# Layer 0's modulation products on TensorE: two steps at a time, eight products in a row

## The chip, the cores and the metric

The kernel runs on one core of a Trainium2 chip. The metric is the device time of one execution in microseconds (us); lower is better. A core has five engines with queues of their own, which run beside each other: TensorE (PE in the profile; its weight loads are PEld), VectorE (DVE), ScalarE (ACT), GpSimd (POOL) and SyncE (SP), which here issues all transfers from HBM. An engine executes its queue in order and waits where an instruction needs something that another engine or a transfer has not finished. The products accumulate in PSUM banks; everything else lies in SBUF.

## What is computed

Two layers of a trunk (pooling mixer, then neighbourhood attention, each followed by a gated MLP with a width-3 convolution) on 256 latent and 256 context tokens of 2048 channels. Each layer is modulated: a matrix of 2048 x 12288 is multiplied with SiLU of a conditioning vector, and the result gives six vectors of 2048 (shift, scale, gate for the mixer and for the MLP):

```python
silu_c, silu_cc = jax.nn.silu(c), jax.nn.silu(c_ctx)
for i in range(DEPTH):                                   # DEPTH = 2
    ml = (silu_c @ w_mod[i] + b_mod[i]).reshape(B, 6, 1, D)
    mc = (silu_cc @ w_mod[i] + b_mod[i]).reshape(6, 1, 1, D)
    a_lat = modulate(rms_norm(h, norm1_g[i]), ml[:, 0], ml[:, 1])
    ...
    h = h + ml[:, 2] * y_lat
    h = h + ml[:, 5] * conv_ffn(modulate(rms_norm(h, norm2_g[i]), ml[:, 3], ml[:, 4]), ...)
```

The change concerns the products `silu_c @ w_mod[0]` and `silu_cc @ w_mod[0]` of layer 0. Layer 1's are made on VectorE (`mod_pairs`, L214) and are not touched.

## The kernel before

**Chunks and steps.** The 12288 columns of a layer's modulation matrix are 24 chunks of 512 columns; chunk ch belongs to vector ch // 4 and to channel group ch % 4. `mod_pe` (L193) computes one chunk of layer 0. It is a generator with four steps g (2048 rows of the matrix are 4 x 4 x 128). In a step, `load` (L123) brings 2048 columns of four row blocks as two transfers of 512 KB each, and four products (L199) follow, one for each row block j. A product has 128 rows, 512 columns of the matrix as moving data, and only 32 columns of stationary data (two are in use, for the latent and the context vector). `tile_position=(0, 32 * j)` puts the four products of a step on the four 32-column strips of TensorE, and their results on the four 32-partition quarters of one PSUM bank; the first transfer of a step serves j = 0 and 1, the second j = 2 and 3. Since the data are 32-bit floats, each product of the source is two records in the trace. After the fourth step ACT copies the bank to SBUF (L204), PE turns it (L209, tile `modt`), DVE adds up the quarters (L211), and `finish_mod` adds the bias. A chunk is called by its number below, a step and transfer as chunk_step: 22_3 are the two transfers of step 3 of chunk 22.

**The order of the chunks.** `mods` (L425) makes, for each channel group g, the chunks g, 4+g, 8+g, 16+g and 12+g, and at last chunks 20 to 23. `need(n)` (L438) drives this generator to step n. Mixer, partial products and modulation of the four groups are interleaved: `mixer(g)` (L446) pools 512 channels on DVE, POOL and ACT and multiplies them with the mixer weights (products `pm`, L490 to L492); `partial(g)` (L516) multiplies these channels with the first eight tiles of layer 0's gate and up weights (products `cg` and `cu`, L551 to L553, for `wcg` and `wcu`; with small products `pwg` and `pwu`, L534, that read the weights as loaded, and their turns `ptg` and `ptu`, L567). While `partial(g)` runs, `between` (L591) calls `need` at a fixed pace and advances `mixer(g + 1)`. After the last group come the gate and up products of tile 8 (`gu0`, L638 to L640, weights `wg_8` and `wu_8`).

**The weights' way.** All weights go through `load`. `split` (L133) then makes two roundings of each for the fp32r products: ACT casts the high part (L145), DVE subtracts it (L147). The modulation products use the loaded tile itself.

**The rooms.** A transfer's tile lies in a room. `stage` (L115) gives rooms in turn: the first of the list is taken and put at its end. Six rooms are always there; `lend` (L111) adds rooms that hold activations later: 12 at first, 8 during groups 0 to 2, and in group 3 four, then none (`LENT`, L41). A transfer into a room waits until the last reader of the room's former content is done. SyncE issues the transfers in one queue and waits in order.

**Who sets the order.** The program is recorded by the Python code and then ordered by the tile framework's scheduler, which estimates times when the program is built and decides the order on each engine; `high_priority` and `issue_after` guide it. So the order in which instructions stand on an engine can change far from an edit. The order is fixed before the program runs.

Of the kernel before, what the change touches and what calls it, by code (L numbers as in the profile page):

```python
# [59 lines left out]
def kernel(ctx: ExitStack, tc: tile.TileContext, xT, cxT, wmod, wg, wu, wd, wp,  # L60
                         wq, wv, wo, vec, cc, rope, inv, strips, out):
    nc = tc.nc
# [8 lines left out]
    def bank(tag, name):  # L71

        if tag == "d" and nbank[0] is not None:
            nbank[0] += 1
            if nbank[0] % 4 == 0:
                tag = "m"
        return pp.tile([P, 512], F32, tag=tag, bufs={"gu": 4, "d": 3, "m": 1}[tag], name=name)
# [37 lines left out]
    def stage(name):  # L115

        r = rooms.pop(0)
        rooms.append(r)
        if r >= 0:
            return ap0.tile([P, 1024], F32, tag=f"A{r}", name=name)  # L120
        return wst.tile([P, 1024], F32, tag=f"wst{-r}", name=name)

    def load(src, cols, name):  # L123

        ts = []
        for j in range(0, cols, 1024):
            n = min(1024, cols - j)
            t = stage(f"{name}_{j}")
            nc.sync.dma_start(t[:, :n], src(j, j + n))
            ts.append((t, n))  # L130
        return ts

# [18 lines left out]
    def ld(src, name, share=0):  # L151
        return split(load(lambda a, b: src[:, a:b], 2048, name), name, share)
# [6 lines left out]
    def mod_tile(l, ch):  # L159

        return main.tile([P, 4, 2], F32, tag=f"modT{ch if ch < 20 else (l, ch)}", name=f"modT{l}_{ch}")

    def by_row(ps):

        return ps.rearrange("p (i j c) -> p i c j", i=4, j=4)[:, :, 0:2, :]
# [9 lines left out]
    def finish_mod(l, ch, streams, src):  # L175

        mt = src[0] if len(src) == 1 else mod_tile(l, ch)
        n = len(streams)
        which, q = divmod(ch, 4)

        def dup(name, a):
            return V(name)[:, a : a + 8].rearrange("p (i s) -> p i s", s=2)[:, :, 0:n]

        bias = dup(f"bm_{l}", 8 * ch)
        for b, v in enumerate(src):
            own = slice(32 * b, 32 * b + 32) if len(src) > 1 else slice(0, P)
            nc.vector.tensor_tensor(mt[own, :, 0:n], v, bias[own], op=ALU.add)
        if which in (1, 4):
            nc.vector.scalar_tensor_tensor(mt[:, :, 0:n], mt[:, :, 0:n], 1.0, dup(f"g{1 if which == 1 else 2}_{l}", 8 * q),
                                           op0=ALU.add, op1=ALU.mult)  # L190
        modT[l, ch] = mt

    def mod_pe(l, ch, sc, pool):  # L193

        ps = bank("m", f"mod{l}_{ch}")
        for g in range(4):
            ts = load(lambda a, b: wmod[l, ch, g, :, a:b], 2048, f"wm{l}_{ch}_{g}")
            for j in range(4):
                nc.tensor.matmul(ps[32 * j : 32 * j + 32, :], sc[:, 4 * g + j, :],  # L199
                                 ts[j // 2][0][:, 512 * (j % 2) : 512 * (j % 2) + 512],  # L200
                                 start=(g == 0), stop=(g == 3), tile_position=(0, 32 * j))
            if g == 3:
                ev = pool.tile([P, 512], F32, tag="t2", name=f"modev{l}_{ch}")
                nc.scalar.copy(ev, ps)  # L204
            yield
        with tc.high_priority():
            p2 = bank("d", f"modt{l}_{ch}")
            for i in range(4):
                nc.tensor.transpose(p2[:, P * i : P * i + P], ev[:, P * i : P * i + P], ident)  # L209
        r = mod_tile(l, ch)  # L210
        nc.vector.tensor_reduce(out=r, in_=by_row(p2), axis=AX.X, op=ALU.add)  # L211
        finish_mod(l, ch, both, [r])
# [116 lines left out]
    with ExitStack() as ph0:  # L329
# [17 lines left out]
        sc = p0.tile([P, KT, 32], F32, name="sc")  # L347
# [44 lines left out]
        with ExitStack() as phs:  # L392
# [16 lines left out]
            for j in range(2):  # L409
                t = st.tile([P, 2, WP], F32, bufs=1, name=f"pad{j}")  # L410
# [3 lines left out]
            for j in range(2):  # L414
                t = st.tile([P, 4, 32], F32, bufs=1, name=f"sh{j}")
# [9 lines left out]
            def mods():  # L425

                for g in range(4):
                    for w in (0, 1, 2, 4):
                        yield from mod_pe(0, 4 * w + g, sc, f0)
                    yield from mod_pe(0, 12 + g, sc, f0)  # L430
                    shifts(g)
                for q in range(4):
                    yield from mod_pe(0, 20 + q, sc, f0)
# [82 lines left out]
            def partial(g, sh, between):  # L516

                step = 0
                for fa in range(0, NS, 4):
                    for q, (nm, wsrc) in enumerate((("g", wg), ("u", wu))):  # L520
                        ts = load(lambda a, b: wsrc[0, fa + a // 512 : fa + b // 512, :, 512 * g : 512 * g + 512]
                                  .rearrange("f p c -> p f c"), 2048, f"wc{nm}{g}_{fa}")
                        parts = split(ts, f"wc{nm}{g}_{fa}")
# [715 lines left out]
```

## Time and profile before

| | |
|---|---|
| runs | 3067.25, 3070.6, 3072.18 us, median 3070.6 |
| the profiled execution's own time | 3070.34 us |
| its span | 3068.5 us |
| mean granted TensorE clock | 0.994 |
| modulation products of layer 0 (L199) | 768 records, 131.1 us of PE's busy time |
| their transfers | 192 of 512 KB |
| idle time of PE before L199 that a transfer ended | 23.3 us |

The span runs from the first to the last instruction of the profiled execution; its own time adds what lies around it. Times in the profile are counted from the span's start. A row of a timeline gives start, duration, engine, line, operation, output <- inputs, shapes, the count of merged records, and in brackets the idle time before it with what ended it. Records of TensorE overlap, since its work is pipelined: the distance between starts says more than the duration.

### The profile page before, as it was taken

The page shows a single profiled execution, that of the slowest core. Times are in us where ns is not written, and L with a number is a line of the kernel's source. Part 1 is how long each engine was busy: PE and PEld are TensorE (multiplying, and loading weights), DVE is VectorE, ACT ScalarE, POOL GpSimd, SP SyncE. Part 2 cuts the span into 40 slices and gives each one's busy share as a digit, 9 for nine tenths or more (in the row PEclk, how much of TensorE's full clock was granted, in tenths as well). Part 3 has the DMA queues.
Part 4 walks back from the last instruction along what each step waited for, and adds up shares of the span by engine and source line. Part 5 has one row for each costly group of instructions (what it writes and reads, how often), then busy time and mean ns, then how long its engine had stood idle before and what let it go on. Part 6 is the DMA issues. An engine that isn't in the chain of part 4 may idle for free.

```text
span 3068.5 us, 40828 instructions
## 1 busy us (share of the span) xinstructions
PE 3007.0 (98%) x15082; PEld 2414.2 (79%) x15082; DVE 1939.4 (63%) x2748; ACT 1372.9 (45%) x2219; POOL 826.4 (27%) x823
## 2 busy tenths in 40 slices
PE   6999999999999999999999999999999999999998
PEld 2565658888888888888887888878888888888887
DVE  4445774285674857658485666474767666666666
ACT  3333454423333242433334444343545666666665
POOL 2011213303022130311302000000002566566665
PEclk9999999999999999999999999999999999999999
DMA  9878663284755747466482333333355556565553
GB/s 382 334 271 305 215 233 103 90 253 141 223 178 180 226 148 250 148 203 202 161 253 83 113 108 104 106 112 106 106 159 184 183 180 201 189 188 180 185 192 117
DMA packets 177927, 559.70 MB, mean 182 GB/s; under 512 B 17600, under 2 KB 22208, under 8 KB 177728
## 3 DMA queue, kind: packets, MB, share of 16 engines
q1 hardware_dynamic: 177728, 557.10, 55.6%
q8 instruction: 119, 1.95, 0.3%
q14 instruction: 80, 0.66, 0.1%
HBM read 554.93 MB, written 2.10 MB: 182 GB/s over the span
## 4 chain that ended last, share of the span: by engine, by line
PE 94%; DVE 2%; POOL 1%; DMA 1%; ACT 1%; issue 1%; SPq 0%; DVEq 0%; ACTq 0%; POOLq 0%
PE g L773 5%; PE u L773 5%; PE d L664 5%; PE d L666 5%; PE d L665 5%; PE d L820 4%; PE g L638 4%; PE g L640 4%; PE g L639 4%; PE u L639 4%; PE u L638 4%; PE u L640 4%; PE mod L199 3%; PE u L776 3%; PE g L776 3%; PE d L824 2%
## 5 line engine op out<-in xcount | busy, mean ns | idle before, releaser
L677 POOL TENSOR_TENSOR hl<-hl,dy 128x256 f32<-128x256 f32 x160 | 146.7, 917 | 943.3 <-ACT dy L676 943.1
L835 POOL TENSOR_TENSOR hl<-hl,dy 128x256 f32<-128x256 f32 x320 | 332.2, 1074 | 188.2 <-ACT dy L833 186.0
L247 DVE SCALAR_TENSOR_TENSOR macc<-wm,sc,macc 128x512 f32<-128x512 f32 (+1 forms) x360 | 328.9, 946 | 70.8 <-DMA wm<-wmod 69.8
L676 ACT ACTIVATE dy<-d,modT 128x256 f32<-128x256 f32 x320 | 133.1, 469 | 187.1 <-PE d L666 172.4
L199 PE MATMUL mod<-wm,sc 128*32 128x512 f32 x768 | 131.1, 617 | 23.3 <-DMA wm<-wmod 23.3
L677 POOL TENSOR_TENSOR hc<-hc,dy 128x256 f32<-128x256 f32 x160 | 129.0, 806 | 0.0
L833 ACT ACTIVATE dy<-d,modT 128x512 f32<-128x512 f32 x160 | 104.5, 684 | 43.0 <-PE d L824 41.5
L147 DVE TENSOR_TENSOR wd_2l<-wd,wd_2h 128x1024 fp32r<-128x1024 f32 (+1 forms) x44 | 54.6, 1247 | 108.8 <-ACT wd_2h L145 107.6
L922 POOL TENSOR_TENSOR rk<-rk,rp 128x256 f32<-128x256 f32 x16 | 13.2, 826 | 365.5 <-DVE rk L921 309.7
L147 DVE TENSOR_TENSOR wd_3l<-wd,wd_3h 128x1024 fp32r<-128x1024 f32 (+1 forms) x44 | 52.0, 1203 | 76.8 <-ACT wd_3h L145 75.5
L147 DVE TENSOR_TENSOR wd_1l<-wd,wd_1h 128x1024 fp32r<-128x1024 f32 (+1 forms) x44 | 53.7, 1225 | 56.4 <-ACT wd_1h L145 56.4
L472 POOL TENSOR_TENSOR pf<-ws,inv 128x256 f32<-128x256 f32 x32 | 27.7, 885 | 220.6 <-PE mod L199 105.0
L199 PEld LDWEIGHTS mod<-wm,sc 128*32 128x32 f32 x768 | 23.7, 110 | 77.4 <-issue 61.5
L145 ACT CAST wd_1h<-wd 128x1024 fp32r<-128x1024 f32 (+1 forms) x44 | 45.3, 1031 | 78.3 <-PE u L639 53.5
L147 DVE TENSOR_TENSOR wd_0l<-wd,wd_0h 128x1024 fp32r<-128x1024 f32 (+1 forms) x44 | 54.7, 1249 | 36.9 <-ACT wd_0h L145 36.9
L1011 ACT ACTIVATE sb<-sb,nm 128x512 f32<-128x512 f32 x64 | 46.1, 722 | 64.3 <-DVE nm L1007 63.1
L799 DVE TENSOR_TENSOR actb<-sgb,actb 128x256 fp32r<-128x256 f32 x43 | 52.8, 1228 | 26.2 <-ACT actb L798 26.2
L145 ACT CAST wd_0h<-wd 128x1024 fp32r<-128x1024 f32 (+1 forms) x44 | 45.2, 1031 | 53.6 <-PE u L773 29.1
L664 PE MATMUL d<-act,wd_2h 128*128 128x512 f32 x172 | 67.2, 391 | 0.0
L666 PE MATMUL d<-act,wd_2l 128*128 128x512 f32 x172 | 67.0, 390 | 0.0
L665 PE MATMUL d<-act,wd_2h 128*128 128x512 f32 x172 | 67.0, 390 | 0.0
L666 PE MATMUL d<-act,wd_3l 128*128 128x512 f32 x172 | 67.0, 390 | 0.0
(1752 smaller groups left out, 9278.0 us busy)
## 6 DMA issues: line engine op xcount, KB each, us to landing
wm<-wmod SPq DMA_DIRECT2D x384, 512.0 KB, 6.1
wd<-wd SPq DMA_DIRECT2D x168, 512.0 KB, 4.4
wg<-wg SPq DMA_DIRECT2D x156, 512.0 KB, 4.7
wu<-wu SPq DMA_DIRECT2D x156, 512.0 KB, 4.5
wv<-wv SPq DMA_DIRECT2D x32, 512.0 KB, 4.0
wk<-wq SPq DMA_DIRECT2D x32, 512.0 KB, 4.1
wq<-wq SPq DMA_DIRECT2D x32, 512.0 KB, 3.6
wo<-wo SPq DMA_DIRECT2D x32, 512.0 KB, 3.9
```

Source lines behind the costliest of these rows:

```text
L147: eng.tensor_tensor(lo[:, :n], t[:, :n], hi[:, :n].bitcast(F32), op=ALU.subtract)
L199: nc.tensor.matmul(ps[32 * j : 32 * j + 32, :], sc[:, 4 * g + j, :], ts[j // 2][0][:, 512 * (j % 2) : 512 * (j % 2) + 512], start=(g == 0) ...
L247: nc.vector.scalar_tensor_tensor(acc[s], v, sc2[:, k, s : s + 1], acc[s], op0=ALU.mult, op1=ALU.add)
L638: nc.tensor.matmul(ps, hi[:, c : c + P], xh, start=(k == 0), stop=False)
L639: nc.tensor.matmul(ps, hi[:, c : c + P], xl, start=False, stop=False)
L640: nc.tensor.matmul(ps, lo[:, c : c + P], xh, start=False, stop=(k == KT - 1))
L664: nc.tensor.matmul(ps, hi[:, o : o + P], xh, start=(i == 0), stop=False)
L665: nc.tensor.matmul(ps, hi[:, o : o + P], xl, start=False, stop=False)
L666: nc.tensor.matmul(ps, lo[:, o : o + P], xh, start=False, stop=(i == n - 1))
L677: nc.gpsimd.tensor_tensor(h_of(s)[:, k, :], h_of(s)[:, k, :], y[:, s], op=ALU.add)
L773: nc.tensor.matmul(ps, hi[:, c : c + P], flat(B[k]), start=(k == 0), stop=False)
L835: nc.gpsimd.tensor_tensor(hl[:, k, :], hl[:, k, :], y[:, q], op=ALU.add)
```

## The change

`load` keeps each transfer it issues in a list. In `mod_pe`, an even step only loads. The odd step after it issues all eight products of both steps: first its own four, then those of the even step, each time in the order j = 2, 3, 0, 1, so that the transfers are used from the last to the first. The first of the eight gets a dependency on all four transfers. The other seven are issued behind it, at high priority, so that nothing stands between them. The number of products, their data and the number of transfers are the same. In the changed program the 96 steps give 48 such groups of eight.

```diff
+    fetched = []
+
     def load(src, cols, name):
...
-            nc.sync.dma_start(t[:, :n], src(j, j + n))
+            fetched.append(nc.sync.dma_start(t[:, :n], src(j, j + n)).ins)
...
         for g in range(4):
             ts = load(lambda a, b: wmod[l, ch, g, :, a:b], 2048, f"wm{l}_{ch}_{g}")
-            for j in range(4):
-                nc.tensor.matmul(ps[32 * j : 32 * j + 32, :], sc[:, 4 * g + j, :],
-                                 ts[j // 2][0][:, 512 * (j % 2) : 512 * (j % 2) + 512],
-                                 start=(g == 0), stop=(g == 3), tile_position=(0, 32 * j))
+            if g % 2 == 0:
+                held, first = ts, fetched[-2:]
+            else:
+                landing = first + fetched[-2:]
+                with ExitStack() as behind:
+                    for n, (gg, tt) in enumerate(((g, ts), (g - 1, held))):
+                        for j in (2, 3, 0, 1):
+                            ins = nc.tensor.matmul(ps[32 * j : 32 * j + 32, :], sc[:, 4 * gg + j, :],
+                                                   tt[j // 2][0][:, 512 * (j % 2) : 512 * (j % 2) + 512],
+                                                   start=(g == 1 and n == 0), stop=(g == 3 and n == 1),
+                                                   tile_position=(0, 32 * j))
+                            if n == 0 and j == 2:
+                                for x in landing:
+                                    tc.add_manual_dep(ins.ins, x.name, mybir.DependencyInfo(
+                                        mybir.DependencyClass.Sync, mybir.DependencyReason.DATA), reason="whole")
+                                behind.enter_context(tc.issue_after(ins.ins))
+                                behind.enter_context(tc.high_priority())
```

## The prediction

> **What bounds the kernel now.** I read the page first (busy time, then the chain that ended last), then the busy time by stage, then the PE timeline inside the one stage that the change touches.
>
> ```profile
> PE 3007.0 (98%) x15082; PEld 2414.2 (79%) x15082; DVE 1939.4 (63%) x2748; ACT 1372.9 (45%) x2219; POOL 826.4 (27%) x823
> PE 94%; DVE 2%; POOL 1%; DMA 1%; ACT 1%; issue 1%; SPq 0%; DVEq 0%; ACTq 0%; POOLq 0%
> ```
>
> TensorE (PE) is busy for 98% of the span and makes 94% of the chain. So time that leaves PE's queue counts, where nothing else is late behind it. The stages, cut at the first mixer product (57.5) and at the first product of layer 0's gate weights (438.6), and the modulation products' own share of the middle one:
>
> ```profile
> 0.00:57.50 57.50, 29.46 (x130) 9.07 (x130) 27.11 (x51) 21.78 (x51) 10.79 (x23) 0.97 0.98 387
> 57.50:438.60 381.10, 375.73 (x2052) 221.90 (x2050) 211.08 (x372) 153.70 (x280) 66.52 (x69) 1.00 0.79 285
> 57.50:438.60 381.10, 109.02 (x670) 20.21 (x668) 0.00 (x0) 1.00 0.79 285
> ```
>
> The columns are PE, PEld, DVE, ACT and POOL busy, clock, DMA share, GB/s (the third row has no ACT and POOL). Up to 57.5 transfers bound it (DMA share 0.98). From 57.5 to 438.6 PE is busy 375.73 of 381.10 us, DVE 55%, the DMA engines 0.79. In that stage the modulation products take 109.02 us of PE. All that follows is untouched by the change and keeps its order but for a few neighbours, so it is shifted as a whole.
>
> **What is removed: half-filled passes on PE.** One trace record is half of a matmul of the source: x4 is a pair (one transfer, two column strips), x8 is all four strips, x16 two steps (an "eight").
>
> ```profile
> 123.48 0.39 PE L553 MATMUL cg<-Ad,wcg_4l 128*128 128x512 f32 x1
> 123.80 1.07 PE L199 MATMUL mod<-wm,sc 128*32 128x512 f32 x8
> 124.79 0.50 PE L551 MATMUL cg<-Ad,wcg_4h 128*128 128x512 f32 x1
> 125.13 0.39 PE L552 MATMUL cg<-Ad,wcg_4h 128*128 128x512 f32 x1
> 125.36 0.39 PE L553 MATMUL cg<-Ad,wcg_4l 128*128 128x512 f32 x1
> ...
> 126.06 0.40 PE L553 MATMUL cg<-Ad,wcg_4l 128*128 128x512 f32 x1
> 126.38 1.05 PE L199 MATMUL mod<-wm,sc 128*32 128x512 f32 x4
> 127.36 0.51 PE L552 MATMUL cg<-Ad,wcg_4h 128*128 128x512 f32 x1
> 127.70 0.40 PE L553 MATMUL cg<-Ad,wcg_4l 128*128 128x512 f32 x1
> ```
> ```profile
> 240.36 0.40 PE L553 MATMUL cu<-Ad,wcu_4l 128*128 128x512 f32 x1
> 240.69 1.92 PE L199 MATMUL mod<-wm,sc 128*32 128x512 f32 x16
> 242.54 0.50 PE L551 MATMUL cu<-Ad,wcu_4h 128*128 128x512 f32 x1
> 242.88 0.40 PE L552 MATMUL cu<-Ad,wcu_4h 128*128 128x512 f32 x1
> ```
>
> Plain products follow each other every 0.23 us (125.13, 125.36). From 123.48 to 125.13 are 1.65 us; two plain steps would be 0.46; so the x8 in between costs 1.19 us. The x4 costs the same: 127.70 - 126.06 - 0.46 = 1.18. A pair by itself takes the place of a full set of four. The x16 costs 242.88 - 240.36 - 0.46 = 2.06. So each set of up to four strips (a slot) is 0.86 us, and entering and leaving a run is 1.19 - 0.86 = 0.33, about 0.165 a side.
>
> Counting both programs' PE order from the first mixer product to the first gate product: before, 78 runs with 109 slots; after, 36 runs (30 of eight, 6 of sixteen) with 84 slots. Slots: 25 x 0.86 = 21.5 us. Borders between the 128-wide products and anything else fall from 168 to 106: 62 x 0.165 = 10.2. **Gross gain 31.7 us**; if every run that disappears is worth its full 0.33 (42 x 0.33 = 13.9), 35.4.
>
> **What is added: a wait for four transfers, and a later release of their buffers.** PE issues in order, so everything behind the first of eight waits with it. The transfers' other end is the room ring: SyncE's queue stands still until PE has freed the room.
>
> ```profile
> SPq L129 <- PE mod L199: 194.7, 70, 11.1
> L129 SPq DMA_DIRECT2D wm<-wmod x4: 328/382/582, 114.2 to 115.6; - x4
> DMA to landing us min/median/max: 4.0/6.1/8.1
> L129 SPq DMA_DIRECT2D wm<-wmod x4: 328/402/642, 204.4 to 205.8; - x4
> DMA to landing us min/median/max: 4.1/5.7/7.3
> L129 SPq DMA_DIRECT2D wm<-wmod x4: 341/382/592, 257.9 to 259.3; - x4
> DMA to landing us min/median/max: 4.2/6.1/8.0
> DMA to landing us min/median/max: 3.5/6.7/11.6
> ```
>
> In three bursts of four, the fourth lands 1.4 + 8.1 = 9.5, 1.4 + 7.3 = 8.7 and 1.4 + 8.0 = 9.4 us after the first was issued; I take 9.0. I laid the changed order of PE beside the ring (each room's last reader, then the eight that needs its next content) and added up the PE work between, at 0.23 a product and the slots above. For most eights it is over 12 us. Nine have 7.5 to 11.3, three of these under 8.5: they may wait a little. I take **2 us** for the middle (0 to 5).
>
> The end of the stage is different. There six rooms are left, and the loads go round them in this order: 22_0, 22_1, 22_2 | 22_3, 23_0, wcu_4 | 23_1, 23_2, 23_3 (chunk_step, two transfers each; wcu_4 is the last weight block of the partial products). So 22_3 needs 22_0's rooms, wcu_4 needs 22_2's, 23_1 needs 22_3's. Before, each pair freed its room alone. After, PE's order is: chunk 22 as one run of sixteen matmuls (both eights), its transposes, ptg, chunk 23's first eight, pwu, the cu products. The second eight of chunk 22 therefore waits for rooms that the first has just freed. The durations:
>
> ```profile
> L145 ACT CAST wcu_4h<-wcu x2: 1037/1042/1047, 415.1 to 417.3; 128x1024 fp32r<-128x1024 f32 x2
> L147 DVE TENSOR_TENSOR wcu_4l<-wcu,wcu_4h x2: 1218/1218/1218, 416.8 to 418.8; 128x1024 fp32r<-128x1024 f32 x2
> 413.88 0.59 ACT L204 COPY modev<-mod 128x512 f32<-128x512 f32 x1 [2.07 <-PE mod L199]
> 393.26 0.66 PE L567 MATMUL ptu<-ident,peu 128*128 128x128 f32 x4
> 393.85 1.09 PE L534 MATMUL pwg<-wcg,sh 128*32 128x256 f32 x16
> ```
>
> From the start of chunk 22's first eight, in us: its halves free their rooms at 1.2 and 2.05. The burst 23_0, 23_0, 22_3, 22_3 is issued from 1.3; the fourth lands at 10.3: PE waits 8.2. The idle core then runs at half clock (rows below), so the second eight takes 3.8, to 14.1; the burst 23_1, 23_1, wcu_4, wcu_4 goes from 12.6. The second of these lands about 4.0 + 1.24 us later (first landing of a burst, spacing of the rows 42.85 and 44.09 below), at 17.9; the transposes (0.59 for the copy, then two of some 0.66) end near 16.3: 1.6 more. The eight of 23 ends at 19.9; the fourth transfer lands at 21.6: 1.7 more. pwu needs 1.1, beside it the cast 1.04: cu starts at 22.7, and the subtraction (1.22) hides under the eight products that need the cast alone. Without waits cu would start at about 8.2 (two eights 3.7, the copy and two transposes 1.7, an eight 1.85, pwu 1.0). Loss 14.5. Behind it wg_8's second half reuses 23_2's room, which the last eight frees just before the gate product: 9 + 1.04 + 1.22 = 11.3 against some 8.5 us of PE work (copy, transposes, 24 products): about 2.5. With 0.5 for chunk 21's second eight: **17.5 us** (12.5 with bursts at 7.3 and full clock; 21 with 9.5 and busy ACT and DVE queues).
>
> **The first stage** I take at 0 (1.4 gained to 2.5 lost). Chunk 4's second eight now follows its last landing, 0.9 us more than a pair, and the first mixer weight stands two transfers further back (2 x 1.24 by the rows' spacing); against that, 1.92 us of chunk 16 no longer stand ahead of the first mixer product.
>
> ```profile
> 42.85 1.05 PE L199 MATMUL mod<-wm,sc 128*32 128x512 f32 x4 [0.20 <-DMA wm<-wmod]
> 44.09 1.05 PE L199 MATMUL mod<-wm,sc 128*32 128x512 f32 x4 [0.18 <-DMA wm<-wmod]
> 54.61 1.11 PE L209 MATMUL modt<-ident,modev 128*128 128x128 f32 x4 [3.20 <-ACT modev L204]
> 55.65 1.92 PE L199 MATMUL mod<-wm,sc 128*32 128x512 f32 x4
> 54.00:58.00 4.00, 3.39 (x10) 1.36 (x11) 2.81 (x7) 0.92 (x3) 1.61 (x2) 0.57 1.02 418
> ```
>
> **Sum**: -31.7 + 2 + 17.5 + 0 = -12.2. The profiled execution took 3070.3 (span 3068.5 and 1.8 around it), 0.3 below the runs' median of 3070.6. **Forecast 3058 us.**
>
> After the idle 3.20 us ahead of 54.61 the granted clock is 0.57, and a pair takes 1.92 us, not 1.05. [...]
>
> **The rivals.**
>
> A, *the end costs little*: the bursts land sooner, or the first eight of 22 is early enough that the waits overlap work. For it: the first of a burst lands in 4 us. Against it: chunk 22's eights stand next to each other in PE's order. Gross 33.5 less 8: 3045 us.
>
> B, *the mixers' chain takes PE's place*. The work between a modulation result and the mixer's products runs over DVE, ACT and POOL and doesn't get shorter.
>
> ```profile
> 220.00:240.00 20.00, 19.89 (x34) 1.00 0.86 296
> ```
>
> For B: DVE is full in this stretch (the one number after the span is its busy time), ahead of the third mixer. Against it: by PE's work, the time from a group's scale result to its last mixer product only falls from 44.8 to 40.3 us in the second group, and the order puts the same modulation products into the gaps between mixers. If half of the 22 us that the first three groups gain is lost so: 3069 us.
>
> C, the other side, *transfers fall behind the ring*: bursts of four behind bursts of four land later than the three quoted. Place: the nine eights with 7.5 to 11.3 us between release and use, and the three at the end. Price: with bursts at 13.0 (the longest landing, 11.6, behind 1.4 of issuing) the nine wait 32 us together and the end 11 more: 3070 - 31.7 + 17.5 + 32 + 11 = 3099 us. It decides from a landing of about 11 us on, where the gain is gone. For it: SyncE already waits 194.7 us for these products, and it is one queue in order. Against it: the stage's DMA share of 0.79 rises only to some 0.84 when the stage gets 20 us shorter.
>
> D, *the clock*: by the row 54.00:58.00 a spell costs (1 - 0.57) x 4 = 1.7 us of PE time. In the transfer-bound first stage an eight needs four transfers (4 x 1.24 = 5.0 us) and 1.92 us of PE, which leaves gaps of 3 us; the end has three more. Five spells beyond the one counted cost 8.5 us: 3067 us. Against it: in the first stage the clock falls once now, with pairs every 1.24 us and a gap of 3.20 ahead, and lost speed there costs only what the transfers don't hide. [...]
>
> That the products aren't held together is excluded by the changed order (no run shorter than eight).
>
> **How the numbers follow.** Forecast (3052 to 3063 as its own range) 0.42; A 0.17; B 0.15; C 0.15; D 0.11. A measurement of this kernel can tell about 0.2% (6 us) from no change. Faster: the forecast and A, 0.59, less a little where the forecast's end term is at 21 and the middle at 5 (3066): 0.57. Within: B, D and that little, 0.27. Slower: C and the far end of B, 0.16. The range runs from A's 3045 to the upper side of B, 3073; outside lie C and a little below A.
>
> **What would show it.** The modulation products' PE time between the first mixer product and the gate product: 109 us before, about 84 x 0.86 + 36 x 0.33 = 84 after; no x4 standing alone; an x16 between plain products still 2.06 us. At the end, one PE idle of about 8 us ahead of chunk 22's second eight, ended by a wm transfer, then two under 3 us. The first gate product comes some 12 us earlier than at 438.6, and everything from it to the end keeps its 2630 us. I am wrong if PE idles for transfers in many places before the end (C), if idle time is ended by ACT or DVE at the mixers (B), if the waits at the end are under 8 us together (A), or if the granted clock is below 1 in more than two places up to 440 (D).

## The result

Twelve runs of each kernel: 3061.3 us median after the change (3060.3 to 3067.1), 3069.2 before (3066.4 to 3072.8). The ratio is 0.9977, 95% interval 0.9968 to 0.9986: 0.23% faster, 3.3 us above the forecast of 3058 and within its range. The profiled execution took 3060.9 us (span 3059.1; before 3068.5). Two executions of the kernels below are far off and left out of the medians and ratios: one of e1 (14193 us, mean granted clock 0.198) and the profiled one of e10 (3727 us, 0.751), so that e10 has no profile to compare.

The page of the changed kernel, busy time and chain of waits. (In it the lines of `mod_pe` have moved: the products are L207, the copy of the bank L219, the transposes L224, the mixer's products L505 to L507, `pwg` L549, cg and cu L566 to L568, the gate product L653.)

```profile
PE 2977.4 (97%) x15082; PEld 2416.9 (79%) x15082; DVE 1939.4 (63%) x2748; ACT 1371.3 (45%) x2219; POOL 829.1 (27%) x823
PE 93%; DMA 2%; DVE 1%; POOL 1%; ACT 1%; issue 1%; SPq 0%; DVEq 0%; ACTq 0%; POOLq 0%
```

PE lost 29.6 us of busy time, but the span fell by only 9.4. So some 20 us of PE's time turned into idle. The rows below show where: busy time by stage after the change, with the columns of the prediction's stage rows (start to first mixer product, to the gate product, to the end).

```profile
0.00:55.60 55.60, 22.77 (x125) 8.83 (x126) 25.57 (x49) 21.66 (x51) 9.18 (x21) 0.93 0.97 386
55.60:428.80 373.20, 352.81 (x2057) 226.33 (x2056) 209.66 (x372) 150.26 (x278) 69.48 (x71) 0.96 0.80 290
428.80:3059.10 2630.30, 2601.83 (x12902) 2181.79 (x12902) 1704.17 (x2329) 1199.43 (x1890) 750.47 (x731) 0.99 0.52 164
```

The modulation products' own share of the middle one:

```profile
55.60:428.80 373.20, 83.19 (x672) 19.01 (x672) 0.00 (x0) 0.96 0.80 290
```

The middle stage cut at each group's first mixer product, and at group 3's second pwg; after, then before:

```profile
55.60:145.20 89.60, 86.50 (x508) 55.32 (x508) 39.51 (x72) 37.45 (x67) 16.11 (x18) 0.97 0.91 344
145.20:230.90 85.70, 84.97 (x514) 54.57 (x513) 44.14 (x79) 30.38 (x54) 12.23 (x16) 1.00 0.86 312
230.90:316.90 86.00, 84.69 (x504) 55.12 (x503) 51.88 (x88) 31.67 (x56) 13.50 (x15) 1.00 0.85 312
316.90:376.30 59.40, 55.43 (x305) 37.02 (x303) 38.87 (x72) 27.14 (x57) 19.84 (x18) 0.94 0.54 197
376.30:428.80 52.50, 41.22 (x231) 24.30 (x229) 35.27 (x63) 23.63 (x45) 7.79 (x5) 0.84 0.68 228
```
```profile
57.50:145.50 88.00, 86.56 (x485) 50.05 (x484) 35.20 (x68) 36.54 (x65) 11.82 (x16) 1.00 0.91 344
145.50:244.00 98.50, 96.97 (x537) 58.69 (x536) 49.70 (x84) 32.80 (x57) 12.75 (x14) 1.00 0.80 276
244.00:333.50 89.50, 89.50 (x501) 54.34 (x500) 51.98 (x89) 31.22 (x55) 14.90 (x16) 1.00 0.82 301
333.50:393.90 60.40, 58.83 (x325) 36.37 (x325) 39.29 (x71) 28.67 (x59) 19.55 (x18) 1.00 0.57 199
393.90:438.60 44.70, 43.86 (x213) 22.44 (x212) 34.90 (x63) 24.47 (x46) 7.51 (x5) 1.00 0.80 274
```

Up to group 3's second pwg the change is 17.6 us ahead (376.3 against 393.9); in the last stretch it gives back 7.8. The granted clock in the three stretches where it is below 1, cut where it is half:

```profile
55.60:60.70 5.10, 5.10 (x14) 4.05 (x14) 2.85 (x8) 0.62 (x1) 1.62 (x2) 0.50 1.02 418
350.80:357.60 6.80, 5.53 (x25) 3.62 (x26) 4.60 (x10) 1.51 (x4) 1.52 (x1) 0.52 0.32 93
395.20:412.30 17.10, 9.67 (x48) 3.39 (x52) 5.24 (x14) 3.16 (x6) 0.00 (x0) 0.51 0.67 229
```

PE was busy 20.3 us at half clock, so about 10.2 us went there. That gives the account of the middle stage: busy time 375.73 to 352.81 is -22.9, and without the 10.2 the PE **work fell by 33.1**; **idle rose by 15.0** (381.10 - 375.73 = 5.4 before, 373.20 - 352.81 = 20.4 after); **half clock cost 10.2**. Sum -7.9, as the stage. The first stage gained 1.9, the rest lost 0.4: -9.4.

Who PE waited for in that stage (sum, times, longest), and PE's timeline at the end:

```profile
PE mod L207 <- DMA wm<-wmod: 8.9, 2, 7.9
PE modt L224 <- ACT modev L219: 6.2, 6, 2.9
PE pwg L549 <- DVE sh L438: 3.4, 1, 3.4
```
```profile
392.13 1.97 SPq L131 DMA_DIRECT2D wm<-wmod  x4
DMA to landing us min/median/max: 4.1/5.7/7.2
```
```profile
391.04 1.92 PE L207 MATMUL mod<-wm,sc 128*32 128x512 f32 x16
400.89 3.64 PE L207 MATMUL mod<-wm,sc 128*32 128x512 f32 x16 [7.93 <-DMA wm<-wmod]
...
408.24 3.64 PE L207 MATMUL mod<-wm,sc 128*32 128x512 f32 x16 [0.96 <-DMA wm<-wmod]
411.67 1.46 PE L549 MATMUL pwu<-wcu,sh 128*32 128x256 f32 x16
413.06 0.50 PE L566 MATMUL cu<-Ad,wcu_4h 128*128 128x512 f32 x1
```

Chunk 22's second eight stands directly behind its first. SyncE issues the four transfers of the burst that it waits for (rows of 392.13; the last at 393.5) only when the first eight frees its rooms, 1.1 us after that eight's start, and the last lands 7.2 us after its issue, at 400.7. So PE waits 7.93 us, and then the second eight runs at half clock, as does chunk 23's first. All other waits for modulation transfers in the stage sum up to 1.0 us.

The waits of `modt` for ACT's copy of the bank rose too. The longest stands in the first group: 2.90 us ahead of 76.42, where the same place had 1.44 before. No experiment here is about it alone.

The wait of 3.42 us for sh is not one for transfers. DVE's timeline just before it:

```profile
346.64 0.18 DVE L226 TENSOR_REDUCE modT<-modt 128x8 f32<-128x32 f32 x1
346.75 1.42 DVE L331 SCALAR_TENSOR_TENSOR nrm<-hl,modT,n2acc 128x256 f32<-128x256 f32 x1
...
350.30 0.15 DVE L189 TENSOR_TENSOR modT<-modT,vt 128x8 f32<-128x8 f32 x1
...
351.76 0.16 DVE L438 COPY sh<-modT 128x8 f32<-128x8 f32 x1
```

Between chunk 15's result (346.64) and the copy that pwg reads (351.76) DVE's queue has the normalisation of the MLP's inputs. Before the change the same pwg waited too, 1.57 us, for ACT; then the clock stayed at 1.00, now half clock follows (350.8 to 357.6).

### The profile page after: what moved, and what is told of

The parts are those of the page before. It is cut to its first block, busy times and chain, and to the rows that moved or that the text cites. A ratio compares the mean times of both kernels' runs of the same rounds, so it can differ in the third digit from the quotient of the medians.

```text
span 3059.1 us, 40876 instructions
## 1 busy us (share of the span) xinstructions
PE 2977.4 (97%) x15082; PEld 2416.9 (79%) x15082; DVE 1939.4 (63%) x2748; ACT 1371.3 (45%) x2219; POOL 829.1 (27%) x823
## 4 chain that ended last, share of the span: by engine, by line
PE 93%; DMA 2%; DVE 1%; POOL 1%; ACT 1%; issue 1%; SPq 0%; DVEq 0%; ACTq 0%; POOLq 0%
PE g L788 5%; PE u L788 5%; PE d L679 5%; PE d L680 5%; PE d L681 5%; PE d L835 4%; PE g L653 4%; PE g L655 4%; PE g L654 4%; PE u L655 4%; PE u L653 4%; PE u L654 4%; PE g L791 3%; PE u L791 3%; PE mod L207 2%; PE d L839 2%
## 5 line engine op out<-in xcount | busy, mean ns | idle before, releaser
L207 PE MATMUL mod<-wm,sc 128*32 128x512 f32 x768 | 98.9, 641 | 15.2 <-DMA wm<-wmod 13.4
L207 PEld LDWEIGHTS mod<-wm,sc 128*32 128x32 f32 x768 | 22.3, 114 | 65.5 <-issue 62.0
L679 PE MATMUL d<-act,wd_0h 128*128 128x512 f32 x172 | 66.9, 389 | 0.0
```

The costliest lines, as they stand in the source:

```text
L679: nc.tensor.matmul(ps, hi[:, o : o + P], xh, start=(i == 0), stop=False)
```

## The experiments

My theory after the result: the work is saved as forecast; what it loses are the room ring at the end, the wait for sh, and half clock behind each idle stretch. Rivals were that the end is bound by its transfers in any order, that switches and not set filling make the price of a pair, and that the clock costs nothing where transfers decide. All kernels start from the changed one. Times are medians; ratios are to the kernel before, timed beside each batch of runs (medians 3069.2 to 3070.5 us), with the 95% interval. So differences of 1 to 2 us between rows are not told apart.

| run | median us | ratio |
|---|---|---|
| changed kernel | 3061.3 | 0.9977 (0.9968 to 0.9986) |
| e1, pairs for chunks 22, 23 | 3059.9 | 0.9970 (0.9959 to 0.9982) |
| e2, fours throughout | 3058.8 | 0.9964 (0.9951 to 0.9976) |
| e3, other order of strips | 3075.2 | 1.0018 (1.0008 to 1.0028) |
| e4, normalisation later | 3059.5 | 0.9968 (0.9957 to 0.9980) |
| e5, two rooms longer | 3059.0 | 0.9970 (0.9959 to 0.9981) |
| e6, pairs for chunks 0, 4, 8, 16 | 3065.6 | 0.9985 (0.9976 to 0.9994) |
| e7, fours from chunk 21, normalisation later | 3053.0 | 0.9946 (0.9932 to 0.9960) |
| e8, idle filled | 3059.4 | 0.9967 (0.9954 to 0.9979) |
| e9, each strip twice in a row | 3073.7 | one run |
| e10, as e7, normalisation half as late | 3053.5 | 0.9942 (0.9929 to 0.9956) |
| e11, fours from chunk 21 alone | 3055.3 | 0.9960 (0.9946 to 0.9973) |

### e1: the end as before

```diff
+            if ch >= 22:
+                for j in range(4):
+                    nc.tensor.matmul(ps[32 * j : 32 * j + 32, :], sc[:, 4 * g + j, :],
+                                     ts[j // 2][0][:, 512 * (j % 2) : 512 * (j % 2) + 512],
+                                     start=(g == 0), stop=(g == 3), tile_position=(0, 32 * j))
-            if g % 2 == 0:
+            elif g % 2 == 0:
                 held, first = ts, fetched[-2:]
```

> Chunks 22 and 23 as before the change (pairs, each waiting for its own transfer), all else as changed; PE's order is the same up to chunk 22. Theory (the room ring at the end): from chunk 22's first product to the first cu product behind pwu the changed kernel took 22.0 us, of which about 13.8 are waits and half clock; they go, and some five half-filled sets (4.3 us) come back: -9.5, so about 3052 us (3049 to 3056), no PE idle over 3 us ahead of chunk 22's products, first gate product near 419. Rival (the end is bound by its transfers however they are waited for): the idle time moves to the pairs and the time stays at 3060 to 3063.

3059.9 us: the theory's number failed. The last stretch, and PE at chunk 22 (L202 are the pairs):

```profile
378.70:429.10 50.40, 45.38 (x229) 23.84 (x228) 37.04 (x65) 25.50 (x47) 6.93 (x5) 0.93 0.79 262
```
```profile
393.35 2.78 PE L202 MATMUL mod<-wm,sc 128*32 128x512 f32 x24
398.59 1.05 PE L202 MATMUL mod<-wm,sc 128*32 128x512 f32 x4 [2.46 <-DMA wm<-wmod]
```

Idle in the stretch fell from 11.3 to 5.0 us, as it should; but busy time rose by 4.2 although less of it is at half clock. I had counted five half-filled sets, 4.3 us; the work rose by some 6. In the kernel before, this stretch is 43.86 us of work and 0.8 of idle. Going back to pairs takes the wait away together with what it was paid for. The rival's time is near, but its reason is not borne out: only 2.46 us of the idle time moved to a pair. The stretch also starts 2.4 us later than in the changed kernel, mostly by a wait of 2.48 us at one eight far ahead of it.

### e2: each step's four by itself

```diff
-            if g % 2 == 0:
-                held, first = ts, fetched[-2:]
-            else:
-                landing = first + fetched[-2:]
+            landing = fetched[-2:]
...
-                    for n, (gg, tt) in enumerate(((g, ts), (g - 1, held))):
-                        for j in (2, 3, 0, 1):
+                for n, j in enumerate((2, 3, 0, 1)):
```

> Each step's four products in a row, the first waiting for the step's own two transfers; no step waits for another's. 62 runs and 83 sets of four from the first mixer product on (kernel before: 78 and 109; changed: 36 and 84). Theory (half-filled sets of strips cost what full ones cost, 0.86 us each, and a run 0.33): 26 x 0.86 + 16 x 0.33 = 27.6 us less PE work than before, and rooms come free sooner than with eights, so that the end loses perhaps 4 us and the clock 3: 3069 - 27.6 + 7 = 3049 us (3045 to 3056), faster than the changed kernel. Rival (what costs is each switch between 32-column and 128-wide products, not the filling): 16 switches of 0.33 to 0.66 us less, 3058 to 3066 us.

```profile
58.00:423.00 365.00, 354.16 (x2051) 220.22 (x2047) 211.61 (x373) 153.89 (x282) 64.25 (x69) 0.99 0.82 298
423.00:3057.00 2634.00, 2605.76 (x12902) 2185.05 (x12902) 1699.86 (x2326) 1198.03 (x1887) 749.40 (x731) 0.99 0.52 163
```

3058.8 us where 3045 to 3056 was expected. The stage gains most of what the theory says: 365.0 us against 381.1 before, 16.1 of 20.6. PE's work falls by some 26 us (27.6 expected), idle is 10.8 (5.4 before). The gate product comes 15.6 us earlier than before (423.0), 5.8 earlier than in the changed kernel. But behind it the rest takes 2634.0 us, 4.1 more than before: the half clock that follows the last idle covers the first gate products, which costs about 2.7; the other 1.4 was not followed.

```profile
421.40:428.20 6.80, 5.92 (x17) 4.41 (x16) 6.32 (x17) 5.17 (x12) 0.00 (x0) 0.51 0.72 290
```

### e4: the copy of sh ahead of the normalisation

```diff
-                    k = (half - NRH) // 2
-                    if g == 3 and 0 <= k < 12 and (half - NRH) % 2 == 0:
+                    k = (half - NRH - 4) // 2
+                    if g == 3 and 0 <= k < 12 and (half - NRH - 4) % 2 == 0:
```

> The changed kernel, with the normalisation of the MLP's inputs in group 3 recorded 4 half-tiles later, so that on DVE the copy of chunk 15's shift (sh) comes straight after its modulation result and not behind four products of that normalisation. PE's order up to the end of the partial products and SyncE's order are the same. Theory: PE's idle of 3.42 us ahead of pwg (ended by DVE's sh) falls under 1 us, the half clock that starts in it at 351 goes too (about 2.9 us of lost PE work): -6 us, 3055 us (3053 to 3058). Rival (the time is given back at the end, where rooms and not PE decide): 3060 to 3062 us with longer idles ahead of chunk 22 and 23.

```profile
316.80:370.90 54.10, 52.71 (x307) 35.57 (x305) 36.19 (x64) 25.86 (x53) 19.76 (x18) 1.00 0.61 219
370.90:424.30 53.40, 40.34 (x229) 23.47 (x229) 38.33 (x71) 25.16 (x49) 7.29 (x5) 0.90 0.68 234
```

In its place the theory is right: the stretch is 54.1 us (changed kernel 59.4), its clock 1.00 (0.94), and PE waits 0.6 us for sh. The end behind it takes 0.9 us more (the gate product now waits 1.89 us for DVE's late) and the rest 1.4 more. The profiled execution is 3.1 us shorter, the median of six runs 1.8, which these runs can't tell from none; 3059.5 us is above the theory's 3053 to 3058.

### e5: two rooms longer

```diff
-LENT = {(2, 31): range(4, 12), (3, 6): range(8, 12), (3, 13): ()}
+LENT = {(2, 31): range(4, 12), (3, 6): range(8, 12), (3, 13): range(10, 12), (3, 18): ()}
```

> The changed kernel with all its eights, but two of the lent rooms (10 and 11) stay with the transfers for five half-tiles longer; so chunk 22's first eight and 21's second stand in PE's order before the last cg products, and chunk 22's second eight no longer waits for rooms that the first has freed just before it. Theory (the ring, not the number four, makes the wait at the end): the 7.93 us idle falls under 3, the clock stays up: 3061 - 8 to 12 = 3051 us (3048 to 3055). Rival (a wait for four transfers at the end costs what it costs, wherever the rooms are): 3059 to 3063 us; or the normalised inputs that need these two rooms come late and the gate products wait for them: the same time with an idle ahead of g.

```profile
393.73 1.92 PE L207 MATMUL mod<-wm,sc 128*32 128x512 f32 x16
...
400.36 2.91 PE L207 MATMUL mod<-wm,sc 128*32 128x512 f32 x16 [2.88 <-DMA wm<-wmod]
...
425.55 0.80 PE L653 MATMUL g<-A,wg_8h 128*128 128x512 f32 x1 [4.61 <-ACT wg_8h L147]
```

The eights are the same, and chunk 22's second (393.73) no longer waits: the 7.93 us were the rooms' and not the number's. But 3059.0 us, not 3051: a wait of 2.88 comes at the next eight, and the gate product waits 4.61 us for its own weights: wg_8 is issued only at 417.15, behind the last eight (415.64), and cast at 424.45 (in the changed kernel its first half is cast at 417.16). Half clock stands at both. The rivals were right on the sum; the second also on the idle ahead of g, but what came late there was a weight and not the normalised inputs.

### e3 and e9: the same eights on the strips in another order

```diff
-                    for n, (gg, tt) in enumerate(((g, ts), (g - 1, held))):
-                        for j in (2, 3, 0, 1):
+                    for h in (2, 0):
+                        for gg, tt in ((g, ts), (g - 1, held)):
+                            for j in (h, h + 1):
```

That is e3. In e9 the strips come as 2, 2, 3, 3, 0, 0, 1, 1, the two steps in turn.

> The changed kernel with the same eights, waits, transfers and places; only the order of the eight products is other: strips 2,3 of one step, 2,3 of the other, then 0,1 and 0,1, where it was 2,3,0,1 and 2,3,0,1. Theory (what costs is a set of strips, and a set only fills with strips that follow each other and differ): each eight goes from two sets to three (2,3 | 2,3,0,1 | 0,1), +0.86 us on each of the 42 eights behind the first mixer product, +36 us of PE work, less some 5 of waits that it covers: 3092 us (3085 to 3100); if pairs never join, four sets: +72 us, 3128. The x16 record group between plain products takes 2.9 us instead of 2.06. Rival (what an isolated pair cost was the switch between kinds of products, not its empty strips): x16 stays at 2.06 us and the time at 3061.

> As e3, but each strip's two products directly behind each other (strips 2,2,3,3,0,0,1,1; outputs unchanged). In e3 the eight with only two different strips in its first four still cost 2.07 us between plain products. Theory now (a run costs 0.33 us and 0.86 for every four products in a row or part of four, whichever strips they are on): x16 again 2.05 to 2.07 us between plain products. Rival (strips do matter, two products on the same strip can only follow each other; e3 hid it because its neighbours differed): 2.9 us or more. The whole time is not what is asked: the rooms are freed in another order, as in e3, so 3070 to 3080.

An eight between plain products in e9:

```profile
142.22 0.39 PE L566 MATMUL cu<-Ad,wcu_4h 128*128 128x512 f32 x1
142.54 1.94 PE L206 MATMUL mod<-wm,sc 128*32 128x512 f32 x16
144.41 0.50 PE L567 MATMUL cu<-Ad,wcu_4l 128*128 128x512 f32 x1
144.75 0.40 PE L565 MATMUL cu<-Ad,wcu_4h 128*128 128x512 f32 x1
```

144.75 - 142.22 - 0.46 = 2.07 us; in e3 ten eights that stand so cost 2.06 or 2.07. My theory of e3 is false: which strips follow each other makes no difference of more than 0.02 us (2.05 in the changed kernel). In the kernel before, a run of one product costs 1.17, of two 1.18, of three 1.19, of four 1.19, of five 2.03, of six 2.04, of seven 2.04, of eight 2.06 (medians of the runs that stand between plain products, with nothing waited for). So the price goes by **the count, in fours**, and a part of four costs a whole one. The rival fell too, since a switch alone would not jump between four and five (1.19 to 2.03). The single records of the traces before and after the change show the same steps: the two records of a product start 0.43 to 0.45 us apart, and up to four products start theirs together (6 to 8 ns from one to the next). So these runs go on in steps of 0.43 us, two for each four products, full or not. A record does not name its strip; how products for the same strip fit in at the same price, in e3 and e9, was not shown.

e3 and e9 are slower than the changed kernel at other places: their transfers stand in another order, and at the end PE idles 10.59 and 4.58 us (e3), 8.74 and 6.18 (e9) ahead of the two eights where it had been 7.93 and 0.96. In e3 another 1.94 us is the wait of group 3's last `pwg` for its weights; the rest was not followed.

### e6: the start as before

```diff
-            if ch >= 22:
+            if ch in (0, 4, 8, 16):
```

(Against e1: the pairs are at the start and not at the end.)

> Chunks 0, 4, 8 and 16 as before the change, the rest as changed: the transfer-bound start with pairs. By stage, the changed kernel gained 33.4 us of PE work between the first mixer product and the gate product and lost 15.0 to idle and 10.2 to half clock, of which 2.6 of half clock and 1.7 of idle stand between the first and the second group's mixer. Theory D (gaps of 3 to 4.5 us between eights at the start make the half clock that reaches into the first mixer): with pairs the half clock in that stretch falls below 1 us; the second mixer starts at about 144 (before 145.5, changed 145.2), 3059 us. Rival (the first stage is bound by transfers and its clock costs nothing): first mixer product back at 57.5, second mixer at 146 to 147, 3062 to 3064.

3065.6 us: the theory fails, and the rival's side is right, though all its numbers are off (3062 to 3064 us, first mixer product at 57.5, second mixer at 146 to 147). Half clock between the first and the second mixer fell from 2.6 to 0.9 us as the theory wanted, but the first mixer product came 1.1 later and the second mixer at 145.7 (changed 145.2). The remaining loss lies in the groups behind it, whose order shifts with the edit; one eight there waits 2.3 us for its transfers. e6 therefore prices the start only roughly.

### e8: work in the idle

```diff
+                if ch == 22 and g == 2:
+                    idle = bank("d", "idle")
...
+                        for _ in range(8):
+                            fill = nc.tensor.matmul(idle, ones, flat(sc), start=True, stop=True)
```

The eight stand behind the first of the chunk's eights and ahead of the second.

> The changed kernel with eight 32-bit products of 128x512 that nobody needs between chunk 22's two eights, where PE stood idle for 7.93 us: some 7.5 us of idle time become work, nothing comes sooner by it. Theory (the granted clock falls because PE stood idle, and the half clock costs time of its own): the spell 395 to 412 goes, the second eight of 22, the first of 23 and pwu take 1.92, 1.92 and 1.1 us instead of 3.64, 3.64 and 1.46: -4 us, 3057 (3056 to 3059). Rival (the clock falls for another reason, or the transfers decide at each of these places so that speed there is worth nothing): 3061 us.

```profile
390.51 1.92 PE L216 MATMUL mod<-wm,sc 128*32 128x512 f32 x16
392.36 7.13 PE L208 MATMUL idle<-sc,ones 128*128 128x512 f32 x16
400.38 1.92 PE L216 MATMUL mod<-wm,sc 128*32 128x512 f32 x16 [0.88 <-DMA wm<-wmod]
...
406.85 1.92 PE L216 MATMUL mod<-wm,sc 128*32 128x512 f32 x16 [2.68 <-DMA wm<-wmod]
409.62 1.09 PE L558 MATMUL pwu<-wcu,sh 128*32 128x256 f32 x16 [0.85 <-DMA wcu<-wu]
410.69 0.50 PE L575 MATMUL cu<-Ad,wcu_4h 128*128 128x512 f32 x1
```

The half clock is gone with the same eights and the same transfers (clock 1.00 from 375.80 to 426.40, where the changed kernel's last stretch has 0.84): the idle caused it. (Eight full-width products take 7.13 us here, eight of 32 columns 1.92.) Two eights and pwu are 1.72 + 1.72 + 0.37 us shorter. But the next eight and pwu then wait 2.68 + 0.85 where it had been 0.96, and cu starts 20.2 us behind the first eight, not 22.0. Of 3.8 us of speed 1.8 remain; the rest was hidden behind transfers. Half the theory, half the rival.

### e7, e10, e11: eights, and fours at the end

```diff
+            if ch >= 21:
+                landing = fetched[-2:]
+                with ExitStack() as behind:
+                    for n, j in enumerate((2, 3, 0, 1)):
...
-            if g % 2 == 0:
+            elif g % 2 == 0:
                 held, first = ts, fetched[-2:]
```

That is e2's four from chunk 21 on. e7 has e4's edit as well, e10 has it with 2 in place of 4, e11 doesn't have it.

> Eights up to chunk 20; from chunk 21 on each step's four by itself, waiting for its own two transfers; and the later normalisation of e4. Theory by stages, from the runs so far: PE work without idle and half clock 306.3 (e4, to the last pwg) + 37.3 (e2, from there) + 1 = 344.6; idle 10.5; half clock 5; from 55 the gate product comes at about 415 (changed kernel 428.8), and the rest takes its 2630 to 2634: 3048 us (3045 to 3053). Rival (the transfers at the end come no sooner, or a half clock behind the stage eats it): gate product at 420 or later, 3054 to 3059.

> As e7 without the later normalisation: the changed kernel with single fours from chunk 21 on and nothing else. It tells how much of e7's 8 us under the changed kernel belongs to the end. Theory (the end's waits are the eights' rooms): idle 10.4 to some 4 and half clock 4.9 to 1 behind the last pwg, so 3061 - 9 = 3052, the sh wait of 3.42 us and its half clock are back, the gate wait is 0.88 again: 3052 to 3055 us. Rival (e7's gain is the normalisation's): 3058 to 3061.

> As e7 (eights to chunk 20, single fours from 21), but with the normalisation only 2 half-tiles later instead of 4. In e7 the gate product waited 4.14 us for DVE's late, before and in the changed kernel 0.88. Theory (DVE has the normalisation to catch up at the end, so half the shift is enough for sh and less of a debt): the wait ahead of the gate product falls to 1 to 2.5 us, the wait for sh stays under 2, no half clock at either: 3050 us (3047 to 3053). Rival (the two only trade): 3053 to 3055.

The end of e7, then of e11:

```profile
397.04 1.74 PE L204 MATMUL mod<-wm,sc 128*32 128x512 f32 x8
...
418.94 0.80 PE L667 MATMUL g<-A,wg_8h 128*128 128x512 f32 x1 [4.14 <-DVE late L390]
```
```profile
378.10:420.00 41.90, 36.28 (x213) 22.05 (x212) 35.40 (x65) 26.40 (x48) 8.48 (x5) 1.00 0.84 290
420.00:3050.70 2630.70, 2603.09 (x12902) 2183.27 (x12902) 1700.07 (x2327) 1197.09 (x1888) 748.60 (x731) 0.99 0.52 163
```

e11, which only has fours at the end, takes 3055.3 us: its last stretch is 41.9 us (changed 52.5), its clock 1.00, its idle 5.6. So most of e7's 8 us under the changed kernel is the end's. The profiled execution is the fastest of e11's five (3052.5 to 3061.8 us); two of the five lie at or above its rival's 3058 to 3061, so the trace speaks against that rival more clearly than the times do. Two fours cost 2.38 us where an eight costs 2.06, and free their rooms at once; it is the pair that costs 1.18 us for half the work. e7 takes 3053.0 us, at the edge of what was expected: the later normalisation wins at sh and loses at the gate product (4.14 us for late, half clock behind it). Part of that loss is not the normalisation's: e11, without it, waits there 2.44 us and not the 0.88 that was expected, since PE arrives earlier. e10 with half the shift is 3053.5: no better. That the two trade, as its rival said, fits the time, but without a profile to compare it is not shown. **e7 and e10 beat both kernels**, by 0.54% and 0.58% of the time before.

## Why the prediction was right, point by point

- **Gross gain 31.7 us: right.** 33.1 measured as work, inside the 31.7 to 35.4 of its two ways of counting. That the modulation products took 83.19 us where 84 was forecast is partly luck: the 109 before and the 83.19 are busy time, the 84 is a price with entering and leaving in it; two eights ran at half clock, and without that the busy time would be some 80. The size of the gain was right for a reason stated wrongly: a pair does take the place of a full set of four, but not because strips stay empty. e3 and e9 filled the same strips differently at the same price (2.07 us an eight, 2.05 in the changed kernel).
- **Wait in the middle, 2 us: too much here, inside its 0 to 5.** This execution has none before chunk 22; e6 and e1 have 2.3 and 2.5 us at one eight.
- **The end, 17.5 us: right in mechanism, a little large.** Forecast: a wait of 8.2, the second eight at 3.8, then waits of 1.6 and 1.7, cu 22.7 us behind the first eight. Measured 7.93, 3.64, 0.96, none, 22.0. The 2.5 for `wg_8` did not come in this kernel (it came as 4.61 in e5). The stretch lost 10.4 of idle and 4.8 of half clock, 15.3.
- **First stage 0: gained 1.9**, a little outside its bounds (1.4 gained to 2.5 lost).
- **What the sum left out: some 10 us.** The wait for sh (idle +2.4 in its stretch, half clock 2.8) and the first group (idle +1.7, most of it the longer wait of `modt` for ACT; half clock 2.5) make 9.4; 0.5 of idle in the two groups between and 0.4 behind the stage come on top. The wait for sh is of rival B's kind, a queue on DVE between a modulation result and PE, though at `pwg` and not at the mixers, and at about half of B's price of 11 us; half clock is rival D's. D's sign, the clock below 1 in more than two places up to 440, was there. It cost 10.2 us in three spells of the stage, of which the forecast had counted the second eight's 1.9: the 8.3 left are D's 8.5, though D did not name the spell at `pwg`. The step that failed is "the idle core then runs at half clock", applied at one place only.
- **The number was near partly by luck.** The errors on the other side (gross +1.4, start +1.9, middle and end +4.2) make 7.5 us and paid for most of this, and so the time fell between the forecast's 3058 and D's 3067.
- **A and C: no.** The end did not come cheaper than 8 us. Transfers landed as before (4.1 to 7.2 us in the burst at the end; 3.6 to 11.6 in the whole stage, before 3.5 to 11.6), and no eight in the middle stood for its transfers longer than 2.5 us.

## What to carry to other kernels

Price a short run of small products by whole fours, as measured here (1.17 to 1.19 us for one to four, 2.03 to 2.06 for five to eight), and take the smallest group that fills one: here four in a row saves some 26 of the 33.1 us of work that eight saves, and holds the buffers of one step and not of two. Where a ring of buffers runs out, look at whether the next group stands directly behind the one that frees its rooms; here that wait belonged to the order and not to the transfers (7.93 us, none in e5). A few us of idle on TensorE cost nearly twice here (3.42 us ahead of pwg, then 2.8 at half clock). Removing one wait often only showed the next: e1, e4, e5 and e8 gave 1.4 to 2.3 us each, where fours at the end gave 6.0 and, with the later normalisation, 8.3.

## What the hardware showed that was not expected

Half clock comes in pieces. Up to the gate product the kernel before has one spell of 3.41 us (from 54.41); the changed kernel has three of 6.83 (from 43.86, 54.09 and 351.06) and one of 17.07 (from 395.43): one, two and five times 3.413. The changed kernel's start on one grid: 54.09, 351.06 and 395.43 lie 87 and 13 times 3.413 us apart. The spell of the kernel before starts 0.31 us off that grid.

The length of an idle stretch alone does not tell in these traces whether half clock follows. The 3.42 us ahead of pwg were followed by it in the changed kernel, e1, e3, e5, e6 and e8 (rows of cg at 0.63 us behind them, 0.39 elsewhere). An idle of 2.90 at 71 to 74 us was followed by it in e1, e2, e4, e5 and e7 (modulation products at 0.15 to 0.21 us a record), but not in the changed kernel, e3 and e8 (0.11). One of 2.46 in e7 and one of 2.68 in e2 were (rows of cu and g at 0.63), one of 2.68 in e8 and one of 2.48 in e1 were not (the eight behind each took 1.92). What decides it was not shown.

Executions of one kernel differ too: e11's run from 3052.5 us at a mean granted clock of 0.992 to 3061.8 at 0.989, the changed kernel's from 3060.3 at 0.990 to 3067.1 at 0.988.
